# Attention weights turned by VectorE in 32x32 blocks after a pass through DRAM, in place of eight TensorE transposes per head

## The chip, the core and the metric

The kernel runs on one core of a Trainium2 chip. TensorE multiplies matrices (PE in the profile, with its weight loads as PEld), VectorE (DVE) and ScalarE (ACT) work on tiles in on-chip memory, GpSimd (POOL) does little here, and SyncE (SP) issues most DMAs. Engines work through their instructions in order and meet by semaphores. An instruction that waits therefore holds everything that stands behind it on its engine, DMAs that this engine issues included. TensorE writes to eight PSUM banks, each 128 partitions by 512 values.

The metric is the device time of one execution in microseconds (us); lower is better. Three runs of the kernel before took 1805.0, 1805.11 and 1809.3 us, so the median is 1805.11 us. The profiled execution is a fourth one.

## The reference

Two layers over 256 latent tokens (a grid of 4 rows by 64) and 256 context tokens, width 2048. The first layer projects the tokens by one large matrix into queries, keys, values, gates and the inputs of a state space model (SSD), lets 16 attention heads and the SSD work beside each other, and projects both results back. The second is a short gated convolution. The change lies in the attention of the first layer:

```python
s_lat = jnp.einsum('bqhd,bkhd->bhqk', qr, kb).astype(jnp.float32) * scale + bias.astype(jnp.float32)
s_lat = jnp.where(mask, s_lat, -jnp.inf)
s_ctx = jnp.einsum('bqhd,bkhd->bhqk', qr, k_ctx).astype(jnp.float32) * scale
pr = jax.nn.softmax(jnp.concatenate([s_lat, s_ctx], axis=-1), axis=-1).astype(v.dtype)
return (jnp.einsum('bhqk,bkhd->bqhd', pr[..., :kh * GRID_W], vb)
        + jnp.einsum('bhqk,bkhd->bqhd', pr[..., kh * GRID_W:], v_ctx))
```

With four grid rows every query sees all 256 latent keys (those out of its column window are masked) and the 256 context keys. So a head has a 256 x 512 matrix of weights. The attention output is then multiplied by a SiLU gate: `ya = ya * jax.nn.silu(...)`.

## The kernel before

**Precision.** A product of two float32 tiles is made of three TensorE matmuls: each operand is split into a rounded high part H (a cast, mostly on ScalarE) and a remainder L (a subtraction on VectorE), and H·H, L·H and H·L are summed in a bank. For the large weights this runs as a stream. SyncE loads 512 KB into one of five `raw` buffers, ScalarE casts it to `wH` (L409), VectorE subtracts to `wL` (L416), TensorE uses both. There are three pairs `wH`/`wL`, so a cast waits until TensorE is done with the chunk three back.

**Order.** The program is written out by a planner in the code: the class `Plan` keeps a clock for each engine, to which the method `cost` adds an estimate for each instruction. Generators (`head_gen`, `kq_gen`, `mix_gen` and others) yield conditions; `may` lets one go on when its inputs are ready by those clocks, when a bank is free (`nb=1`), and when the budget of ten `tmp` tiles of 128x512 and nine `half` tiles allows it (`grow` asks for tiles, `cap` gives the claim back). The planner fixes only the order in which each engine gets its instructions and which buffer they use; on the chip each starts when its real inputs are there. The conditions named "AQ" stand for DMAs that ScalarE issues (`DMA2`).

**The projections.** Columns of the input projection come in four groups `a`, each with K, Q, G (gate) and V of four heads, and between them the SSD groups with columns B, C, X and Z. The SSD columns go through `conv`: one activation from the bank (L1194), four multiply-adds on VectorE that read the same bank (L1200), a tanh (L1203) and a last multiply-add (L1207). `kq_gen` normalises K and Q into six `tmp` tiles and then turns each by four TensorE transposes into a bank (`turn`, L202); ScalarE copies the four turned K tiles to `KT` (L962), VectorE the two of Q to `QT` (L964). It does the turning for group `a` only when `attn[0] >= 8 * a`, that is, when all heads of the earlier groups are done, because there is one `KT` and one `QT`. V and G wait for the same in their banks.

**A head.** `head_gen(a, h)` splits K and Q, makes two score tiles (128 queries by 512 keys each), adds the bias and takes the row maximum (`top`), applies the exponential on ScalarE with the row sum, and scales by 0.5 over the sum on VectorE (`scale_`, L1028 and L1029). Then the weights are turned, since the next product sums over keys: `trans` makes four TensorE transposes per score tile into a bank, ScalarE casts the bank to half of `PH` (L1065), VectorE subtracts to half of `PL` (L1067). After the split of V (`vH`, and `vL` in L1076) twelve matmuls of 256 columns sum the head's output (the PV product below), VectorE multiplies by the gate (L1087), and `put_mix` writes the result to DRAM by a DMA that ScalarE issues (L921).

**The output projection.** `mix_gen` reads two heads back from DRAM (L1516), splits them (L1521, L1522), and the output projection uses them as `mix0` to `mix31` (16 attention heads, 16 halves of the SSD). Heads 12 to 15 are the last ones that it uses, `mix12` to `mix15`.

## Time and profile before

| Quantity | Value |
| --- | --- |
| Median of three runs | 1805.11 us |
| Profiled execution, its own time | 1800.62 us |
| Span of that profile | 1798.8 us |
| Granted TensorE clock, mean | 0.999 |
| TensorE matmuls on `tmp` tiles by L202 (transposes) | 324 |
| of these in the attention heads, 16 x 8 | 128 |
| ScalarE busy, share of the span | 44% |
| VectorE busy, share of the span | 72% |

The span goes from the first to the last instruction; the rest of the execution's time, 1.8 us, lies around it. A busy time is a sum of durations on the engine, with overlapping ones counted once. A matmul's duration runs from its start to its modelled end and overlaps the next one's, so the pace of TensorE is read from starts, not from means. "Idle before" is the time in which the engine had nothing to do ahead of a group, with what ended it.

The attention lies between about 200 and 1240 us of the span.

### The profile page before, as it was taken

What the parts mean: (1) busy time and instruction counts of PE and PEld (TensorE: products, weight loads), DVE (VectorE), ACT (ScalarE), POOL (GpSimd) and SP (SyncE); (2) the same over time, 40 slices, a digit from 0 to 9 for tenths busy, and PEclk for the clock granted to TensorE, in tenths of its full rate; (3) what the DMA queues carried; (4) which work ended last, traced back from release to release, by engine and by line L of the source; (5) the groups of instructions that cost most, each with busy time, mean ns of one, the idle gap of its engine ahead of it and who ended that gap; (6) DMA issues with size and microseconds to landing.
All of it is one profiled execution on the core that took longest, in us unless ns stands there. A gap on an engine that the chain in (4) does not pass through costs nothing.

```text
span 1798.8 us, 26647 instructions
## 1 busy us (share of the span) xinstructions
PE 1765.1 (98%) x10057; PEld 1493.6 (83%) x10057; DVE 1302.0 (72%) x2121; ACT 796.7 (44%) x1410; POOL 31.1 (2%) x28
## 2 busy tenths in 40 slices
PE   6999999999999999999999999999999999999998
PEld 4677888888888879888888898888878888888887
DVE  5566777878686877685875787787657777777665
ACT  5322544436252455242454343654445444444442
POOL 0000100001000000000001000000000000000000
PEclk9999999999999999999999999999999999999999
DMA  9987654566656556655574566878857777877564
GB/s 343 343 289 256 194 168 126 156 205 196 201 171 190 156 184 200 191 157 167 171 218 119 163 190 194 233 218 286 282 182 229 242 247 226 263 224 247 188 210 153
DMA packets 249217, 376.92 MB, mean 210 GB/s; under 512 B 32656, under 2 KB 104048, under 8 KB 249088
## 3 DMA queue, kind: packets, MB, share of 16 engines
q1 hardware_dynamic: 239792, 366.64, 65.5%
q10 hardware_dynamic: 9296, 8.57, 1.4%
q8 instruction: 79, 1.29, 0.3%
q14 instruction: 50, 0.41, 0.1%
HBM read 368.70 MB, written 7.77 MB: 209 GB/s over the span
## 4 chain that ended last, share of the span: by engine, by line
PE 91%; DMA 3%; DVE 3%; issue 1%; ACT 1%; SPq 0%; POOL 0%; POOLq 0%; DVEq 0%; ACTq 0%
PE bank L198 89%; PE bank L202 3%; DMA tmp<-dram_csr 2%; DVE wL L416 1%; DMA raw<-in_ada_w 0%; DMA tmp<-dram_mixd 0%; DVE acc L803 0%; DMA tmp<-in_x 0%; DVE hL L752 0%; SPq L566 0%; DVE tmp L1381 0%; DVE tmp L1200 0%; ACT wH L409 0%; DVE half L1396 0%; DVE tmp L748 0%
## 5 line engine op out<-in xcount | busy, mean ns | idle before, releaser
L409 ACT CAST wH<-raw 128x1024 fp32r<-128x1024 f32 (+1 forms) x440 | 459.1, 1044 | 684.7 <-PE bank L198 585.5
L416 DVE TENSOR_TENSOR wL<-raw,wH 128x1024 fp32r<-128x1024 f32 (+1 forms) x440 | 531.9, 1214 | 227.0 <-ACT wH L409 224.3
L198 PE MATMUL bank<-h,wH 128*128 128x512 f32 x1024 | 358.7, 395 | 2.7 <-ACT h L1664 1.5
L198 PE MATMUL bank<-hH,wH 128*128 128x256 f32 (+1 forms) x1040 | 343.2, 330 | 0.9 <-ACT wH L409 0.9
L198 PE MATMUL bank<-hL,wH 128*128 128x256 f32 (+1 forms) x1040 | 337.2, 324 | 0.0
L198 PE MATMUL bank<-hH,wL 128*128 128x256 f32 (+1 forms) x1024 | 331.7, 324 | 1.1 <-DVE wL L416 1.1
L198 PE MATMUL bank<-h,wL 128*128 128x256 f32 x1024 | 287.2, 280 | 0.1
L198 PE MATMUL bank<-wH,hH 128*128 128x512 f32 x640 | 257.4, 403 | 4.8 <-ACT hH L746 2.6
L198 PE MATMUL bank<-wL,hH 128*128 128x512 f32 x640 | 250.1, 391 | 0.3 <-DVE wL L416 0.3
L198 PE MATMUL bank<-wH,hL 128*128 128x512 f32 x640 | 249.8, 391 | 0.1
L803 DVE SCALAR_TENSOR_TENSOR acc<-raw,csil,acc 128x512 f32<-128x512 f32 x256 | 191.8, 749 | 59.8 <-DMA raw<-in_ada_w 45.4
L198 PEld LDWEIGHTS bank<-h,wH 128*128 128x128 f32 x1024 | 192.2, 188 | 48.4 <-issue 2.6
L198 PEld LDWEIGHTS bank<-hH,wH 128*128 128x128 f32 x1040 | 197.9, 190 | 18.7 <-issue 2.0
L198 PEld LDWEIGHTS bank<-hL,wH 128*128 128x128 f32 x1040 | 198.0, 190 | 15.4
L198 PEld LDWEIGHTS bank<-hH,wL 128*128 128x128 f32 x1024 | 194.8, 190 | 17.5 <-DVE wL L416 2.1
L198 PEld LDWEIGHTS bank<-h,wL 128*128 128x128 f32 x1024 | 193.6, 189 | 0.4 <-DVE wL L416 0.4
L198 PE MATMUL bank<-wH,mix 128*128 128x512 f32 x512 | 162.8, 393 | 0.0
L198 PEld LDWEIGHTS bank<-wH,hH 128*128 128x128 f32 x640 | 120.3, 188 | 35.3 <-issue 6.6
L198 PEld LDWEIGHTS bank<-wH,hL 128*128 128x128 f32 x640 | 120.2, 188 | 25.4 <-DVE hL L752 0.6
L198 PEld LDWEIGHTS bank<-wL,hH 128*128 128x128 f32 x640 | 120.3, 188 | 24.6 <-DVE wL L416 1.1
L198 PEld LDWEIGHTS bank<-wH,mix 128*128 128x128 f32 x512 | 96.2, 188 | 20.7 <-issue 0.9
L198 PE MATMUL bank<-wL,mix 128*128 128x512 f32 x256 | 99.9, 390 | 0.0
(259 smaller groups left out, 1790.1 us busy)
## 6 DMA issues: line engine op xcount, KB each, us to landing
raw<-in_w_in SPq DMA_DIRECT2D x209, 512.0 KB
raw<-in_ada_w SPq DMA_DIRECT2D x163, 512.0 KB
raw<-in_sc_in SPq DMA_DIRECT2D x128, 512.0 KB
raw<-in_w_out SPq DMA_DIRECT2D x64, 512.0 KB
raw<-in_sc_out SPq DMA_DIRECT2D x32, 512.0 KB
tmp<-dram_csr SPq DMA_DIRECT2D x32, 256.0 KB
PT<-in_ada_w SPq DMA_DIRECT2D x14, 512.0 KB
yi<-in_ada_w SPq DMA_DIRECT2D x8, 512.0 KB
```

The lines of the kernel that those rows point to most:

```text
L198: E(T.matmul(o, l, r, start=start, stop=stop, skip_group_check=True))
L202: E(T.transpose(o, i, ident if k == 128 else ident[:k, :k]))
L409: E(S.copy(H, v))
L416: E(V.tensor_tensor(out=Lo, in0=v, in1=H.bitcast(F32), op=ALU.subtract))
L803: E(V.scalar_tensor_tensor(out=acc, in0=v[:, j], scalar=csil[:, 2 * k + j:2 * k + j + 1], in1=acc, op0=ALU.mult, op1=ALU.add))
```

## The change

Per head, the eight transposes, the bank they took, two casts and two subtractions go. In their place:

- The exponential writes into a new `tmp` tile with its columns in another order (`mixed`): the columns of key block k, 32-wide piece b, move so that DRAM rows can be read in whole pieces of 128 values.
- The scaling goes from VectorE to ScalarE (`S.mul`), and its factor 0.5 goes into the gate multiplication, now a `scalar_tensor_tensor`.
- ScalarE's queue writes each scaled tile to DRAM (`ptd`, 256 KB, two per head). `fetch` reads them back with four DMAs, each to 32 partitions, eight pieces of 512 bytes for each partition: 4 x 32 x 8 = 1024 pieces per head.
- `blocks` turns the fetched tile by a VectorE transpose that works in 32x32 blocks, two instructions of 128x512 per head, into `Pf`.
- One cast of 128x1024 makes `PH`, one subtraction of 128x1024 makes `PL`.
- A head asks for three `tmp` tiles rather than two, and gives its claim back before the fetch rather than after the turning.
- The planner's cost list treats the new transpose like a reduction.

```diff
-            if op in ("Reciprocal", "TensorReduce"):
+            if op in ("Reciprocal", "TensorReduce", "StreamTranspose"):
...
+    mixed = lambda ap: ap.rearrange("p (b k i) -> p k b i", b=4, k=4)
+    plain = lambda ap: ap.rearrange("p (k b i) -> p k b i", b=4, k=4)
+
+    def fetch(dst, src):
+
+        n = src.shape[0] // 32
+        for b in range(4):
+            E(DMA2.dma_start(dst[32 * b:32 * b + 32].rearrange("p t (a x) -> p (t a) x", a=4),
+                             bass.AP(tensor=src.tensor, offset=src.offset + 128 * b, ap=[[512, 32], [32 * 512, n], [1, 128]])))
+
+    def blocks(o, i):
+
+        E(V.transpose(o.rearrange("p k (a j) -> p a k j", a=4), i.rearrange("p (a k j) -> p a k j", a=4, k=4)))
...
-    PH, PL = (st([128, 4, 256], f"PT{k}", F32R, name=f"P{'HL'[k]}") for k in range(2))
+    PH = st([128, 4, 256], "PH", F32R)
+    Pf = st([128, 4, 256], "PT1", name="Pf")
+    ptd = drt([16, 256, 512], "ptd")
...
-            E(S.activation(sp, sp, AF.Exp, bias=s4[:, 2 + qt:3 + qt], scale=1.0, accum_out=s4[:, 4 + qt:5 + qt]))
+            ex = sps[qt] = tmp()
+            E(S.activation(mixed(ex), plain(sp), AF.Exp, bias=s4[:, 2 + qt:3 + qt], scale=1.0, accum_out=s4[:, 4 + qt:5 + qt]))
+            give(free_t, sp)
 
         def scale_(qt):
-            sp = sps[qt]
+            yield W_("DVE", s4[:, 4 + qt:5 + qt])
             E(V.reciprocal(s4[:, 6 + qt:7 + qt], s4[:, 4 + qt:5 + qt]))
-            E(V.tensor_scalar(out=sp, in0=sp, scalar1=s4[:, 6 + qt:7 + qt], scalar2=0.5, op0=ALU.mult, op1=ALU.mult))
-
-        def trans(qt):
-            pt = bank()
-            for kt in range(4):
-                turn(pt[:, kt * 128:(kt + 1) * 128], sps[qt][:, kt * 128:(kt + 1) * 128])
+            yield W_("ACT", s4[:, 6 + qt:7 + qt])
+            E(S.mul(sps[qt], sps[qt], s4[:, 6 + qt:7 + qt]))
+            yield W_("AQ", sps[qt])
+            E(DMA2.dma_start(ptd[hd, qt * 128:(qt + 1) * 128], sps[qt]))
             give(free_t, sps[qt])
-            return pt
...
-        yield ("grow", 2, 0)
+        yield ("grow", 3, 0)
...
+        for qt in range(2):
+            yield from scale_(qt)
+        yield ("cap", 0, 0)
         yield when(lambda: hd == 0 or ("pv", hd - 1) in got)
+        yield W_("AQ", ptd[hd])
+        Dt = st([128, 2, 512], "PT0", name=f"D{hd}")
+        fetch(Dt, ptd[hd])
         for qt in range(2):
-            yield W_("PE", sps[qt], nb=1)
-            pt = trans(qt)
-            t = slice(qt * 128, (qt + 1) * 128)
-            yield W_("ACT", pt)
-            E(S.copy(PH[:, :, t], four(pt)))
-            yield W_("DVE", PH[:, :, t])
-            E(V.tensor_tensor(out=PL[:, :, t], in0=four(pt), in1=PH[:, :, t].bitcast(F32), op=ALU.subtract))
-            give(free_b, pt)
-        yield ("cap", 0, 0)
+            yield W_("DVE", Dt)
+            blocks(Pf[:, :, qt * 128:(qt + 1) * 128], Dt[:, qt])
+        yield W_("ACT", Pf)
+        E(S.copy(PH, Pf))
+        yield W_("DVE", PH)
+        PL = st([128, 4, 256], "PT0", F32R, name=f"PL{hd}")
+        E(V.tensor_tensor(out=PL, in0=Pf, in1=PH.bitcast(F32), op=ALU.subtract))
...
-            E(V.tensor_tensor(out=o, in0=po[:, :256], in1=gt[:, h, :], op=ALU.mult))
+            E(V.scalar_tensor_tensor(out=o, in0=po[:, :256], scalar=0.5, in1=gt[:, h, :], op0=ALU.mult, op1=ALU.mult))
```

The planner writes another order with these estimates. Three places show it. Line numbers after the change are 14 or 15 higher at these places (before L409, L416, L921, L962, L1194, L1516; after L423, L430, L935, L976, L1209, L1531).

**First place: the end of head 3 and the turning of K and Q for the second group.** TensorE, before: `tmp` tiles are turned in banks 4, 7 and 1, each its own, with matmuls of the projection between (`hH10`, `hL10` are the split activations, `wH2`, `wL2` the split weights).

```order
L202 MATMUL bank4_127<-const_153,tmp7_111 128x128 x4
L198 MATMUL bank6_129<-hH10_1128,wH2_138 128x256
L198 MATMUL bank6_129<-hL10_1133,wH2_138 128x256
L198 MATMUL bank6_129<-hH10_1128,wL2_141 128x256
L198 MATMUL bank6_129<-hH10_1128,wH2_138 128x256
L198 MATMUL bank6_129<-hL10_1133,wH2_138 128x256
L198 MATMUL bank6_129<-hH10_1128,wL2_141 128x256
L202 MATMUL bank7_130<-const_153,tmp8_112 128x128 x4
L202 MATMUL bank1_124<-const_153,tmp4_108 128x128 x4
L198 MATMUL bank0_123<-hH11_1135,wH2_138 128x256
```

TensorE, after: the last rows of head 3's PV product (`PH`, `PL3`, `vH`, `vL`), the six turnings, and the first rows of the next projection.

```order
L198 MATMUL bank3_126<-PH_1685,vH_1690 128x256
L198 MATMUL bank3_126<-PL3_4050,vH_1690 128x256
L198 MATMUL bank3_126<-PH_1685,vL_1691 128x256
L202 MATMUL bank3_126<-const_153,tmp1_105 128x128 x4
L202 MATMUL bank3_126<-const_153,tmp2_106 128x128 x4
L202 MATMUL bank3_126<-const_153,tmp8_112 128x128 x4
L202 MATMUL bank3_126<-const_153,tmp4_108 128x128 x4
L202 MATMUL bank3_126<-const_153,tmp0_104 128x128 x4
L202 MATMUL bank3_126<-const_153,tmp7_111 128x128 x4
L198 MATMUL bank3_126<-hH0_360,wH2_138 128x256
```

The turnings now stand in one row with nothing between, all six in bank 3, directly behind head 3's PV product, which is in bank 3 too; the matmuls that stood between them come earlier.

VectorE, after, around the same place: the multiply-adds of `conv` read banks 3 and 7 (L1215), `half2` is head 3's gate multiplication (L1102), `QT` the copies of turned Q.

```order
L1215 SCALAR_TENSOR_TENSOR tmp5_109<-bank3_126,cwh_1672,tmp5_109 128x2x254
L430 TENSOR_TENSOR wL1_140<-raw0_131,wH1_137 128x1024
L1215 SCALAR_TENSOR_TENSOR tmp5_109<-bank3_126,cwh_1672,tmp5_109 128x2x255 x2
L1215 SCALAR_TENSOR_TENSOR tmp5_109<-bank3_126,cwh_1672,tmp5_109 128x2x254
L1222 SCALAR_TENSOR_TENSOR tmp5_109<-tmp6_110,tmp5_109 128x512
L1215 SCALAR_TENSOR_TENSOR tmp3_107<-bank7_130,cwh_1672,tmp3_107 128x2x254
L1215 SCALAR_TENSOR_TENSOR tmp3_107<-bank7_130,cwh_1672,tmp3_107 128x2x255 x2
L1215 SCALAR_TENSOR_TENSOR tmp3_107<-bank7_130,cwh_1672,tmp3_107 128x2x254
L1102 SCALAR_TENSOR_TENSOR half2_116<-bank3_126,gt_145 128x256
L978 TENSOR_SCALAR QT_143<-bank3_126,gqk_1678 128x4x128 x2
```

Head 3's product, the gate and the turnings follow a `conv` whose input lies in the same bank 3; ScalarE has ahead of that `conv` a cast to `wH1`, and behind it the tanh, the activation from bank 7 and the four copies to `KT`, in this order:

```order
L423 CAST wH1_137<-raw0_131 128x1024
L1209 ACTIVATE tmp5_109<-bank3_126,cbh_1674,cwh_1672 128x512
L1218 ACTIVATE tmp6_110<-tmp5_109 128x512
L1209 ACTIVATE tmp3_107<-bank7_130,cbh_1674,cwh_1672 128x512
L976 COPY KT_142<-bank3_126 128x4x128 x4
```

Before, casts of weights stood between those copies, which came from banks 1, 4, 7 and 1.

**Second place: the turning for the third group.** TensorE, after: head 7's PV product ends in bank 3, the two tiles of Q are turned in banks 5 and 3, and an SSD product uses bank 5 next.

```order
L198 MATMUL bank3_126<-PL7_5645,vH_1690 128x256
L198 MATMUL bank3_126<-PH_1685,vL_1691 128x256
L202 MATMUL bank5_128<-const_153,tmp1_105 128x128 x4
L202 MATMUL bank3_126<-const_153,tmp3_107 128x128 x4
L198 MATMUL bank5_128<-tmp8_112,xtm_147 64x128
```

The four tiles of K follow a little later, in banks 2 and 7 by turns.

```order
L198 MATMUL bank0_123<-wH1_137,hL0_364 128x512
L202 MATMUL bank2_125<-const_153,tmp7_111 128x128 x4
L202 MATMUL bank7_130<-const_153,tmp2_106 128x128 x4
L202 MATMUL bank2_125<-const_153,tmp1_105 128x128 x4
L202 MATMUL bank7_130<-const_153,tmp0_104 128x128 x4
L198 MATMUL bank4_127<-wH1_137,hH0_360 128x512
```

Before, the four tiles of K of this group were turned in banks 3, 4, 7 and 3, with matmuls of the projection between the first three.

**Third place: head 15 and the end of the output projection.** TensorE, before: the last rows of head 15's product stand ahead of `mix18`.

```order
L198 MATMUL bank5_128<-PH_1685,vH_1689 128x256
L198 MATMUL bank5_128<-PL_1686,vH_1689 128x256
L198 MATMUL bank5_128<-PH_1685,vL_1690 128x256
L198 MATMUL bank2_125<-wH1_137,mix18_9245 128x512
L198 MATMUL bank2_125<-wL1_140,mix18_9245 128x512
```

TensorE, after: the last rows of the same product, whose twelve rows follow directly on the last matmul on `mix13`, and the first rows on `mix14`, which is head 14 and, like `mix15`, comes back by the read that also waits for head 15.

```order
L198 MATMUL bank0_123<-PH_1685,vH_1690 128x256
L198 MATMUL bank0_123<-PL15_10046,vH_1690 128x256
L198 MATMUL bank0_123<-PH_1685,vL_1691 128x256
L198 MATMUL bank4_127<-wH2_138,mix14_10067 128x512
L198 MATMUL bank4_127<-wL2_141,mix14_10067 128x512
```

ScalarE, after: the fetch of head 15 (`D15` from `ptd`), four casts of weights, the split of the turned weights and of V, the write of head 15's result and the read of both heads.

```order
L212 DMA D15_9972<-dram_ptd_1687 32x8x128 x4
L423 CAST wH1_137<-raw4_135 128x1024
L423 CAST wH2_138<-raw1_132 128x1024
L423 CAST wH0_136<-raw3_134 128x1024
L423 CAST wH1_137<-raw2_133 128x1024
L1081 CAST PH_1685<-Pf_1686 128x1024
L1089 CAST vH_1690<-Vt_144 128x512
L935 DMA dram_mixd_1684<-half5_119 128x256
L1531 DMA tmp5_109<-dram_mixd_1684 128x2x256
L1536 CAST mix14_10067<-tmp5_109 128x256
```

Head 15 has moved from well ahead in the output projection to the place right in front of its first use; between its product and that use nothing is left on TensorE.

More of the change, by code (lines that the diff above doesn't have):

```diff
@@ L1054, in head_gen @@
         yield from top(1, p1)
-        yield W_("DVE", sps[0])
-        scale_(0)
-        yield W_("DVE", sps[1])
-        scale_(1)
+        for qt in range(2):
+            yield from scale_(qt)
+        yield ("cap", 0, 0)
         yield when(lambda: hd == 0 or ("pv", hd - 1) in got)
+        yield W_("AQ", ptd[hd])
+        Dt = st([128, 2, 512], "PT0", name=f"D{hd}")
+        fetch(Dt, ptd[hd])
         for qt in range(2):
-            yield W_("PE", sps[qt], nb=1)
-            pt = trans(qt)
-            t = slice(qt * 128, (qt + 1) * 128)
-            yield W_("ACT", pt)
-            E(S.copy(PH[:, :, t], four(pt)))
-            yield W_("DVE", PH[:, :, t])
-            E(V.tensor_tensor(out=PL[:, :, t], in0=four(pt), in1=PH[:, :, t].bitcast(F32), op=ALU.subtract))
-            give(free_b, pt)
-        yield ("cap", 0, 0)
+            yield W_("DVE", Dt)
[5 more added lines that the diff above has]
+        E(V.tensor_tensor(out=PL, in0=Pf, in1=PH.bitcast(F32), op=ALU.subtract))
         yield when(lambda: ("V", a) in got and ("G", a) in got)
```

## The prediction

> **What bounds the kernel now.** The busy times come first, at the head of the page; of a row, the busy us, the share of the span and the instructions:

> ```profile
> PE 1765.1 (98%) x10057; PEld 1493.6 (83%) x10057; DVE 1302.0 (72%) x2121; ACT 796.7 (44%) x1410; POOL 31.1 (2%) x28
> ```

> TensorE is busy for 98%. Next, the view by windows, for the stretch in which the attention lies; after the length come busy us of PE, PEld, DVE, ACT and POOL, the granted clock, the DMA share and GB/s.

> ```profile
> 200.00:1240.00 1040.00, 1036.40 (x5938) 892.42 (x5937) 784.28 (x1344) 468.63 (x929) 27.04 (x16) 1.00 0.62 186
> ```

> Here TensorE lacks 3.6 us of 1040. So in this stretch every us of TensorE work that goes is a us won, as long as nothing makes TensorE wait, and every wait of TensorE is lost in full: there is no slack to take it back. ScalarE (469 us busy) and VectorE (784 us) have room on average. Whether TensorE waits is decided by the order in single places.

> **What the change removes.** The chain of waits in order of time (start, us, what) shows what a transpose costs; below it the group of all transposes of `tmp` tiles (busy us, mean ns of one, then idle before).

> ```profile
> 15.82 4.57 PE bank L202 x32
> ...
> 276.26 0.87 PE bank L202 x8
> ...
> L202 PE MATMUL bank<-const,tmp 128*128 128x128 f32 x324 | 45.9, 273 | 0.2 <-ACT KT L962 0.2
> ```

> The mean of 273 ns is a duration up to a modelled end and overlaps its neighbours; a row of eight takes 0.87 us, 109 ns each. For 16 heads with 8 transposes each that is 128 x 109 ns = **14.0 us** less. [...]

> **What it adds beside TensorE.** The groups by form, with mean ns of one behind the busy us:

> ```profile
> L416 DVE TENSOR_TENSOR wL<-raw,wH 128x1024 fp32r<-128x1024 f32 x433 | 527.0, 1222 | 226.3 <-ACT wH L409 223.6
> L409 ACT CAST wH<-raw 128x1024 fp32r<-128x1024 f32 x433 | 454.8, 1051 | 666.9 <-PE bank L198 573.8 <-issue 58.2 <-DMA bias<-dram_rpbs 5.7
> L1067 DVE TENSOR_TENSOR PL<-bank,PH 128x512 fp32r<-128x512 f32 x32 | 21.9, 686 | 6.1 <-ACT PH L1065 5.7
> L1065 ACT CAST PH<-bank 128x512 fp32r<-128x512 f32 x32 | 18.2, 586 | 30.5 <-PE bank L202 29.0 <-DVE half L1087 1.5
> L1029 DVE TENSOR_SCALAR tmp<-tmp,s 128x512 f32<-128x512 f32 x32 | 15.6, 487 | 1.1
> L596 ACT ACTIVATE xs<-xs,rx 128x512 f32<-128x512 f32 x8 | 5.4, 716 | 5.8 <-POOL rx L555 5.8
> L793 DVE MEMSET acc<- 128x512 f32 x16 | 7.8, 485 | 0.9
> L964 DVE TENSOR_SCALAR QT<-bank,gqk 128x512 f32<-128x512 f32 x8 | 5.8, 747 | 2.2 <-PE bank L202 2.2
> ```

> The issue rows of ScalarE's writes and SyncE's small-piece reads give min, median and max ns of issuing:

> ```profile
> L921 ACTq DMA_DIRECT2D dram_mixd<-half x32: 321/328/623, 285.9 to 1217.5; - x32
> ...
> L1001 SPq DMA_DIRECT2D bias<-dram_rpbs x64: 573/614/1828, 229.1 to 1166.3; - x64
> ```

> The block transpose of 128x512 is in no row. The cheapest and the dearest VectorE pass of that size shown here take 0.485 (a fill) and 0.747 us (from a bank); I take 0.6, between them, as it reads on-chip memory. VectorE per head: minus 2 x 0.487 (scaling) and 2 x 0.686 (`PL` halves), plus 1.222 (`PL` whole) and 2 x 0.6, so +0.1 us. ScalarE per head: plus 2 x 0.716 (scaling), 1.051 (cast), 2 x 0.328 (writes), 4 x 0.614 (fetch), minus 2 x 0.586, so +4.4 us, 71 us in all, on an engine with 571 us free in the stretch. Both I cost at nothing: casts of weights mostly wait for TensorE (574 of 667 idle us in L409's row), so this work fits into waits. If that cover were gone for a head, up to 4.4 us would show there. The trip through DRAM lies between scores and product, where TensorE has tens of us of projection for most heads.

> **First stop: head 3's product and the turning for the second group.** The order puts the product, then all six turnings in bank 3, with nothing between; the bank's earlier user is a `conv`. More groups, then TensorE's timeline at head 15's product, and the gate on VectorE behind it:

> ```profile
> L1194 ACT ACTIVATE tmp<-bank,cbh,cwh 128x512 f32<-128x512 f32 x24 | 18.0, 767 | 0.0
> L1200 DVE SCALAR_TENSOR_TENSOR tmp<-bank,cwh,tmp 128x510 f32<-128x510 f32 x48 | 35.9, 747 | 1.3
> L1200 DVE SCALAR_TENSOR_TENSOR tmp<-bank,cwh,tmp 128x508 f32<-128x508 f32 x48 | 35.4, 744 | 3.6 <-ACT tmp L1194 3.1
> L1203 ACT ACTIVATE tmp<-tmp 128x512 f32<-128x512 f32 x24 | 15.1, 629 | 7.0 <-DVE tmp L1200 7.0
> L1207 DVE SCALAR_TENSOR_TENSOR tmp<-tmp,tmp 128x512 f32<-128x512 f32 x24 | 16.4, 684 | 0.0
> L1087 DVE TENSOR_TENSOR half<-bank,gt 128x256 f32<-128x256 f32 x16 | 6.7, 422 | 9.7 <-PE bank L198 9.7
> L962 ACT COPY KT<-bank 128x512 f32<-128x512 f32 x16 | 8.9, 589 | 8.7 <-PE bank L202 8.7
> ```

> ```profile
> 1195.65 0.28 PE L198 MATMUL bank<-PH,vH 128*128 128x256 f32 x1
> ...
> 1196.94 0.28 PE L198 MATMUL bank<-PH,vL 128*128 128x256 f32 x1
> 1197.05 0.40 PE L198 MATMUL bank<-wH,mix 128*128 128x512 f32 x1
> ```

> ```profile
> 1197.43 0.42 DVE L1087 TENSOR_TENSOR half<-bank,gt 128x256 f32<-128x256 f32 x1
> ```

> The twelve rows of a product take 1197.05 - 1195.65 = 1.40 us. Let TensorE reach head 3's product at 0, when it has just freed `wH1`. ScalarE's queue then has the cast (to 1.05) and the activation of `conv` (to 1.82); VectorE does one multiply-add (to 2.56), `wL1` (to 3.78) and three more (2 x 0.747 + 0.744, to 6.02). With 0.2 for handovers bank 3 is free at 6.2. Then the tanh (0.63), the last multiply-add of `conv` (0.68) and, beside it, the activation from bank 7 (0.77), four multiply-adds (2.98) and the gate (0.42) follow, for the gate stands behind them on VectorE: 11.2. The product itself lies beside these. The six turnings are one chain, since each needs the bank back: 6 x 0.44 on TensorE, 2 x 0.747 and 4 x 0.589 for the copies, together 6.5, and handovers of 0.27 each, taken between nothing and the 0.49 us from the product's last start (1196.94) to the gate's (1197.43): 8.1, end at 19.3. TensorE works for 1.40 + 2.62 of it, so it stands for **15.3 us** (bounds 13.5 to 16.7 by the handovers). Before, the turnings used several banks and had projection between them, so all this was hidden. What is queued behind: the casts for the next weights, which TensorE needs only after the stop.

> **Third group.** Head 7's product is followed by Q's turnings in banks 5 and 3 and an SSD product in bank 5. Bank 3 waits for the gate (0.49 - 0.12 + 0.42 behind the product, less the 0.44 of the other turning: 0.4), bank 5 for gate and copy on VectorE: 1.0 more. K's tiles alternate between two banks and lose about 0.4 twice. Together **2.2 us**, between 0 and 4.4.

> **Second stop: head 15 ahead of `mix14`.** The rows of ScalarE's timeline give the latency of a read-back, from issue to the first cast, at three places, and the write of head 15:

> ```profile
> 1103.67 0.37 ACTq L1516 DMA_DIRECT2D tmp<-dram_mixd  x1
> ...
> 1106.33 0.71 ACT L1521 CAST mix<-tmp 128x256 fp32r<-128x256 f32 x2 [0.55 <-DMA tmp<-dram_mixd]
> ...
> 1142.89 0.41 ACTq L1516 DMA_DIRECT2D tmp<-dram_mixd  x1
> ...
> 1147.14 0.71 ACT L1521 CAST mix<-tmp 128x256 fp32r<-128x256 f32 x2 [0.31 <-DMA tmp<-dram_mixd]
> ...
> 1199.33 0.34 ACTq L921 DMA_DIRECT2D dram_mixd<-half  x1
> ...
> 1209.22 0.38 ACTq L1516 DMA_DIRECT2D tmp<-dram_mixd  x1
> ...
> 1216.98 0.41 ACT L1521 CAST mix<-tmp 128x256 fp32r<-128x256 f32 x1 [4.37 <-DMA tmp<-dram_mixd]
> ```

> ```profile
> L1076 DVE TENSOR_TENSOR vL<-Vt,vH 128x512 fp32r<-128x512 f32 x16 | 10.9, 684 | 0.1
> L1521 ACT CAST mix<-tmp 128x256 fp32r<-128x256 f32 x32 | 11.1, 402 | 10.5 <-DMA tmp<-dram_mixd 10.5
> ```

> The latencies are 2.7, 4.3 and 7.8 us. Before, head 15's write stood 10 us ahead of the read, and TensorE had other halves to work on. After, TensorE reaches head 15's product at 0 having just freed `wH1`: cast (to 1.05), `wL1` (to 2.27) with `PH`'s cast beside it, `PL` (to 3.49), `vL` (to 4.17), with handovers 4.5. Product 1.40 (to 5.9), handover and gate 0.8 (6.7), issue of the write 0.33, its landing, the read, the cast 0.40. A write's landing is in no row; I take the shortest read, 2.7, between nothing and 4.3. With a read of 4.3 the first matmul on `mix14` starts at 14.3, and TensorE stands for 14.3 - 1.4 = **12.9 us** (8.7 with no landing and a read of 2.7; 18.0 with 4.3 and 7.8).

> **Work behind a stop.** The chain's first row above has 32 transposes in 4.57 us, right after TensorE's wait at the start; at 109 ns they would take 3.49. So a long wait costs 1.1 us afterwards; for two stops **2.2 us**, between 0 and the rival below.

> **Sum.** -14.0 + 15.3 + 2.2 + 12.9 + 2.2 = +18.6 us on the profiled execution's own 1800.62, so 1819.2. The median of the runs lies 4.5 above that execution; against the median the forecast is **1823.7 us**. Its own bounds (each term's, most of them at once being unlikely) give 1816 to 1830.

> **Rivals.**

> - *TensorE works slowly through the stops.* Products and turnings inside them are 1.40 + 2.62 + 1.40 = 5.4 us of work; at half pace they add 5.4: 1829.1. For it: the slow start-up row. Against it: the granted clock is 1.00 in the window, though its idle time, 3.6 us in all, hardly tries it. [...]
> - *The fetched pieces come late.* 1024 pieces per head, on queues busy with weights; with 7.8 instead of 4.3 us VectorE waits at the block transposes, `wL` is queued behind them and TensorE waits for it. At two heads with little room (15, whose product has 8 to 10 us of TensorE work behind its fetch, and one more) that is 2 x 3.5: 1830.7. For it: the 7.8 us read. Against it: most heads have over 12 us there (both counted in the new order at this profile's pace of TensorE).
> - *One stop only.* If ScalarE and VectorE are so far ahead that the second stop is hidden, 12.9 + 1.1 fall away: 1809.7. Within 0.3% of the median (5.4 us, about what a measurement of this kernel can tell from no change) is where all stops together cost 8.6 to 19.4 us.
> - *Faster.* The planner's rows only set an order. If `conv` and the gate are done when TensorE arrives, because TensorE is later there than the planner thinks, the stops vanish: 1805.1 - 14.0 = 1791.1. It decides below 8.6 us of stops. For it: L1087's gate waits for TensorE in most of its idle time. Against it: the cast to `wH1` can't start before TensorE frees that buffer, so the chain of the first stop can't run ahead.
> - *The removal pays nothing*, as the transposes filled gaps anyway: 1837.7. Against it: 3.6 us idle in 1040.

> **Chances.** Forecast 0.48, slow work 0.17, late pieces 0.13, one stop 0.12, faster 0.07, no pay 0.03. Faster by over 0.3%: 0.07; within: 0.12; slower: 0.81. The range 1810 to 1837 takes in the first three cases with their bounds and leaves out the most of the others.

> **What would show it.** Transposes of `tmp` tiles: 196 rather than 324. At the first stop an idle time of about 6 us before the product and gaps of near 1 us between six turnings. Idle time of about 8 us before the first `mix14`, with a read-back ahead of it. A block transpose near 0.6 us, hardly any wait for `ptd` on VectorE. A clock below 1.00 behind the stops would speak for slow work. Wrong is the prediction if the turnings run without gaps, or if TensorE's idle time is spread over many heads.

## The result, and the profile after

The changed kernel took 1835.72 us (median of four runs, 1834.53 to 1839.31); the kernel before, run beside it, 1807.2 us. The ratio is 1.016 with a 95% interval of 1.014 to 1.0179: 28.5 us slower. The forecast was +18.6 us, 1823.7. The profiled executions lie a little further apart: 1835.04 and 1800.62 us, with spans of 1833.2 and 1798.8.

The head of the page after:

```profile
span 1833.2 us, 26538 instructions
...
PE 1766.5 (96%) x9929; PEld 1486.6 (81%) x9929; DVE 1301.6 (71%) x2105; ACT 814.1 (44%) x1426; POOL 36.5 (2%) x28
```

TensorE has 128 matmuls fewer (9929 for 10057) and yet 1.4 us more busy time, and its idle time went from 1798.8 - 1765.1 = 33.7 to 1833.2 - 1766.5 = 66.7 us. So two things are to be found: where 33.0 us of new idle time lie, and why its work takes longer in busy time by some 15 us than the removed transposes allow. (A busy time counts each matmul to its modelled end, so some of the latter are ends that overlap nothing now.)

The windows view answers the first. Of the kernel before, three stretches (length, then busy us of PE, PEld, DVE, ACT, POOL, granted clock, DMA share, GB/s):

```profile
450.00:550.00 100.00, 100.00 (x533) 85.03 (x532) 76.14 (x123) 38.70 (x62) 0.00 (x0) 1.00 0.60 183
700.00:750.00 50.00, 50.00 (x278) 42.96 (x277) 34.37 (x59) 19.40 (x30) 0.00 (x0) 1.00 0.56 172
1150.00:1300.00 150.00, 150.00 (x719) 124.18 (x718) 115.58 (x176) 76.38 (x118) 1.43 (x2) 1.00 0.79 256
```

The same stretches of the changed kernel:

```profile
450.00:550.00 100.00, 87.58 (x433) 72.65 (x432) 57.58 (x97) 36.99 (x59) 1.61 (x1) 0.88 0.49 147
700.00:750.00 50.00, 44.52 (x304) 38.25 (x304) 45.06 (x91) 31.82 (x90) 4.75 (x3) 1.00 0.65 187
1150.00:1300.00 150.00, 135.36 (x620) 109.94 (x619) 104.13 (x171) 72.73 (x121) 2.26 (x2) 0.95 0.75 237
```

12.4, 5.5 and 14.6 us of idle time, 32.5 of the 33.0, lie in three stretches: the three places of the order that the prediction named. In two of them the granted clock is down as well (0.88 and 0.95).

**The first stop**, TensorE's timeline (start, us, what; in brackets the idle time before and what ended it):

```profile
502.01 0.39 PE L198 MATMUL bank<-hH,wL 128*128 128x512 f32 x1
508.22 0.55 PE L198 MATMUL bank<-PH,vH 128*128 128x256 f32 x1 [5.82 <-DVE tmp L1215]
508.57 0.41 PE L198 MATMUL bank<-PL,vH 128*128 128x256 f32 x1
508.78 0.41 PE L198 MATMUL bank<-PH,vL 128*128 128x256 f32 x1
...
512.98 1.11 PE L202 MATMUL bank<-const,tmp 128*128 128x128 f32 x4 [1.86 <-DVE half L1102]
514.94 1.12 PE L202 MATMUL bank<-const,tmp 128*128 128x128 f32 x4 [0.84 <-DVE QT L978]
...
518.69 1.12 PE L202 MATMUL bank<-const,tmp 128*128 128x128 f32 x4 [0.68 <-ACT KT L976]
...
524.07 0.58 PE L198 MATMUL bank<-hH,wH 128*128 128x256 f32 x1 [0.68 <-ACT KT L976]
```

And the granted clock in it, from the windows view:

```profile
508.30:513.00 4.70, 2.83 (x13) 2.54 (x13) 3.99 (x6) 1.16 (x2) 0.00 (x0) 0.50 0.42 114
...
524.00:528.00 4.00, 3.93 (x18) 3.93 (x19) 1.68 (x3) 4.00 (x10) 0.00 (x0) 0.50 0.09 33
528.00:532.00 4.00, 4.00 (x37) 3.63 (x35) 1.24 (x3) 2.73 (x6) 0.00 (x0) 0.87 0.00 0
```

This is the predicted chain: the product waits 5.8 us for the last multiply-add of `conv` in its bank, the first turning for the gate, each next one for the copy out of the same bank. What the forecast had too small is the pace. A product's matmuls start 0.21 us apart instead of 0.12, four transposes, 0.44 us by their pace before, take 1.11 up to their modelled end, and the clock stays at 0.50 until about 5 us after work has become continuous again at 524.07 (0.87 as the mean of 528 to 532 us puts its return at 529).

**The last stop**, pieces of the chain of waits in order of time:

```profile
1244.89 5.28 DMA dram_mixd<-half
...
1250.19 0.31 ACTq L212
...
1250.54 8.84 DMA D<-dram_ptd
...
1264.37 2.51 PE bank L198 x10
...
1267.36 1.69 DMA dram_mixd<-half
...
1269.07 3.44 DMA tmp<-dram_mixd
```

The pieces of the last of head 15's four fetch DMAs land 8.84 us after that DMA was issued. TensorE is done with `mix13` at 1258.43 and waits for them and for the block transposes, the cast and the subtraction behind them; then the product, the gate, the write and the read of the result follow one by one. The first two lines say that the third DMA of that fetch went out only when the write of an earlier result had landed.

One wait was in no term of the sum. These are SyncE's and ScalarE's timelines around the fetch of head 14 (what is issued on their queues is marked SPq and ACTq), and the row of all issues of the fetch (min, median and max ns):

```profile
1218.78 0.37 SPq L393 DMA_DIRECT2D raw<-in_w_out  x1
...
1219.72 1.64 ACTq L212 DMA_DIRECT2D D<-dram_ptd  x3
...
1227.42 0.31 ACTq L212 DMA_DIRECT2D D<-dram_ptd  x1
1227.83 1.04 ACT L423 CAST wH<-raw 128x1024 fp32r<-128x1024 f32 x1 [7.12 <-PE bank L198]
...
L212 ACTq DMA_DIRECT2D D<-dram_ptd x64: 309/462/1648, 280.2 to 1250.5; - x64
```

Three of the four DMAs go out in 1.64 us. The fourth starts 6.06 us later, and the cast to `wH` stands behind it on ScalarE. It isn't the issuing that takes long: no issue of the fetch takes more than 1.65 us. By the semaphore events in the trace, the fourth DMA waits for the very semaphore that will tell of its own landing, and that one was still counting the weights that SyncE had asked for at 1218.78. They had landed at 1227.40, 22 ns before the fourth DMA started. (The view puts the cast's wait down to TensorE, but the next cast follows without a wait, so buffers were free.) TensorE then stood for 1.14 and 0.76 us. In three more places, not counting this one, the waits view puts casts down to the fetch directly (us in total, times, longest):

```profile
ACT wH L423 <- DMA D<-dram_ptd: 18.0, 3, 7.9
```

### The profile page after: what moved, and what is told of

Read it like the earlier page. It is cut to its first block, busy times and chain, and to the rows that moved or that the text cites. A ratio compares the mean times of both kernels' runs of the same rounds, so it can differ in the third digit from the quotient of the medians.

```text
span 1833.2 us, 26538 instructions
## 1 busy us (share of the span) xinstructions
PE 1766.5 (96%) x9929; PEld 1486.6 (81%) x9929; DVE 1301.6 (71%) x2105; ACT 814.1 (44%) x1426; POOL 36.5 (2%) x28
## 4 chain that ended last, share of the span: by engine, by line
PE 89%; DMA 4%; DVE 4%; ACT 1%; issue 1%; POOL 0%; ACTq 0%; SPq 0%; DVEq 0%; POOLq 0%
PE bank L198 87%; PE bank L202 2%; DVE wL L430 1%; DMA D<-dram_ptd 1%; DMA raw<-in_ada_w 1%; DMA dram_mixd<-half 0%; ACT wH L423 0%; DMA tmp<-dram_csr 0%; DVE acc L817 0%; DMA raw<-in_w_in 0%; POOL statk L569 0%; DMA raw<-in_w_out 0%; DVE tmp L1215 0%; DMA xs<-in_x 0%; DVE hL L766 0%
## 5 line engine op out<-in xcount | busy, mean ns | idle before, releaser
L423 ACT CAST wH<-raw 128x1024 fp32r<-128x1024 f32 (+1 forms) x440 | 458.6, 1044 | 689.0 <-PE bank L198 540.9
L430 DVE TENSOR_TENSOR wL<-raw,wH 128x1024 fp32r<-128x1024 f32 (+1 forms) x440 | 530.4, 1212 | 223.4 <-ACT wH L423 214.2
L198 PE MATMUL bank<-h,wH 128*128 128x512 f32 x1024 | 360.4, 397 | 2.6 <-ACT h L1679 1.5
L198 PE MATMUL bank<-hH,wH 128*128 128x256 f32 (+1 forms) x1040 | 341.9, 329 | 1.6 <-ACT wH L423 0.9
L198 PE MATMUL bank<-hL,wH 128*128 128x256 f32 (+1 forms) x1040 | 337.8, 325 | 0.0
L198 PE MATMUL bank<-hH,wL 128*128 128x256 f32 (+1 forms) x1024 | 332.2, 324 | 3.9 <-DVE wL L430 3.9
L198 PE MATMUL bank<-h,wL 128*128 128x256 f32 x1024 | 286.3, 280 | 0.4 <-DVE wL L430 0.4
L198 PE MATMUL bank<-wH,hH 128*128 128x512 f32 x640 | 257.1, 402 | 6.7 <-ACT hH L760 2.6
L198 PE MATMUL bank<-wL,hH 128*128 128x512 f32 x640 | 249.9, 391 | 1.0 <-DVE wL L430 1.0
L198 PE MATMUL bank<-wH,hL 128*128 128x512 f32 x640 | 249.7, 391 | 0.1
L198 PEld LDWEIGHTS bank<-h,wH 128*128 128x128 f32 x1024 | 192.2, 188 | 50.8 <-issue 2.6
L198 PEld LDWEIGHTS bank<-hH,wH 128*128 128x128 f32 x1040 | 198.8, 191 | 20.0 <-issue 2.3
L198 PEld LDWEIGHTS bank<-hH,wL 128*128 128x128 f32 x1024 | 195.6, 191 | 20.5 <-DVE wL L430 5.3
L198 PEld LDWEIGHTS bank<-hL,wH 128*128 128x128 f32 x1040 | 198.9, 191 | 15.5
L198 PEld LDWEIGHTS bank<-h,wL 128*128 128x128 f32 x1024 | 193.0, 188 | 0.7 <-DVE wL L430 0.7
L198 PE MATMUL bank<-wH,mix 128*128 128x512 f32 x512 | 162.9, 394 | 8.7 <-ACT mix L1536 7.6
L198 PEld LDWEIGHTS bank<-wH,hH 128*128 128x128 f32 x640 | 120.2, 188 | 37.6 <-issue 6.1
L198 PEld LDWEIGHTS bank<-wL,hH 128*128 128x128 f32 x640 | 120.2, 188 | 26.2 <-DVE wL L430 2.5
L198 PEld LDWEIGHTS bank<-wH,hL 128*128 128x128 f32 x640 | 120.1, 188 | 25.6 <-DVE hL L766 0.6
L198 PEld LDWEIGHTS bank<-wH,mix 128*128 128x128 f32 x512 | 96.9, 189 | 30.6 <-ACT mix L1536 8.3
L198 PE MATMUL bank<-wL,mix 128*128 128x512 f32 x256 | 100.6, 393 | 1.1 <-DVE wL L430 1.1
```

The source lines that it names most:

```text
L198: E(T.matmul(o, l, r, start=start, stop=stop, skip_group_check=True))
L423: E(S.copy(H, v))
L430: E(V.tensor_tensor(out=Lo, in0=v, in1=H.bitcast(F32), op=ALU.subtract))
```

## The experiments

The theory: the order that the planner wrote makes TensorE stop in those three places, and these stops, with the slow clock in and behind them, are the loss. The main rival: the transfers themselves (their pieces, their landing, their issue on ScalarE) cost the time wherever they stand. All ratios below are to the kernel before, which ran beside each group (medians 1805 to 1807).

| Run | Median us | Ratio (95%) |
| --- | --- | --- |
| changed kernel | 1835.72 | 1.016 (1.014 to 1.0179) |
| landing estimate altered | 1831.0 | 1.0125 (1.0101 to 1.0148) |
| and earlier start of scores | 1820.15 | 1.007 (1.0047 to 1.0092) |
| before, transposes doubled | 1813.45 | 1.0038 (1.0026 to 1.0051) |
| changed, useless matmuls in the last stop | 1834.04 | 1.0152 (1.013 to 1.0173) |
| changed, without the trip | 1810.55 | 1.0026 (1.0012 to 1.0039) |
| fetch issued by GpSimd | 1867.85 | 1.0348 (1.0312 to 1.0383) |
| before, heads planned late | 1856.88 | 1.0271 (1.0237 to 1.0304) |
| changed, late results not through DRAM | 1820.97 | 1.0071 (1.0049 to 1.0093) |
| three edits together | 1813.98 | 1.0035 (1.0021 to 1.0049) |
| before, late results not through DRAM | 1805.85 | 0.9993 (0.998 to 1.0007) |
| changed, late results direct, heads first | 1808.83 | 1.0018 (0.9999 to 1.0038) |
| late results direct, landing estimate altered | 1829.6 | 1.0125 (1.0109 to 1.0141) |

**The last stop.** The edit, in the method that writes a head's or an SSD half's result:

```diff
     def put_mix(i, o):
+        if free_rows[0] > i % 16:
+            yield W_("ACT", o)
+            split_mix(i, o)
+            give(free_h, o)
+            written.add(i)
+            return
         yield W_("AQ", o)
```

`split_mix` makes the cast and the subtraction of `mix_gen`, now from the half tile on chip. On the changed kernel:

> The changed kernel, with one edit at its end: results that are ready once the activations' rows are free (heads 12 to 15 and late SSD halves) are split straight from their half tile into the mix tile, without the write to DRAM and the read back. In the changed kernel's chain that pair of DMAs takes 1.69 + 3.44 us between head 15's gate and the split, and the earlier pair held ScalarE too. Theory (the last stop's greater part is this read-back directly ahead of its use): the idle time ahead of mix14 falls from 6.4 us to about 1.5, its slow clock behind goes: 6 to 10 us less, 1826 to 1830. Rival (TensorE is held there by the weights, not by the read-back): within 3 us of 1835.7.

The same edit on the kernel before, as a control:

> The kernel before with the same edit at its end alone (no read-back for late results). It has no stop there, so the theory expects no change: 1803 to 1809. If it becomes faster by more than 5 us, the edit helps by itself and is no measure of the last stop.

14.75 us went, half again the most that was expected, and the control did not move. The stretch that had 14.6 us of idle time has 4.8, with the clock at 1.00:

```profile
1150.00:1300.00 150.00, 145.22 (x681) 119.22 (x681) 112.12 (x178) 79.68 (x127) 1.83 (x2) 1.00 0.79 250
```

So the way of late results through DRAM is the greater part of the last stop, the slow clock included. That is more than the read-back alone: the write that held head 15's fetch went too, and with it TensorE's wait ahead of that head's product. The two parts aren't told apart.

**The first and the middle stop.** One more edit on that kernel:

```diff
         if s:
+            if s < 3:
+                force(lambda: attn[0] >= 8 * s)
             psB = banks(2)
             proj(256, 512, psB, 1)
```

> The kernel of the run without the read-back of late results, with one more edit: before the projection of the SSD columns B of groups 1 and 2 takes its two banks, what is left of the heads of the group ahead is written out. Head 3's product then stands at 430 us of TensorE work instead of 451, ahead of that projection and of its conv, and the six turnings of K and Q alternate between banks 7 and 3. Theory (the first stop is the conv in the same bank and the one bank for six turnings): of 19.5 us lost between 500 and 550 us some 2 to 5 remain, of 7.6 between 700 and 750 some 2: 1821.0 - 20 = about 1801 us (1796 to 1808), at or below the kernel before. Rival (head 3's data are not there earlier, so TensorE waits for the fetch at the new place instead): 1815 to 1825.

12.1 us went. The median, 1808.83, is just above the theory's range, and can't be told from the kernel before. The same two stretches:

```profile
450.00:550.00 100.00, 94.81 (x489) 78.72 (x489) 69.18 (x114) 41.75 (x65) 1.61 (x1) 0.97 0.63 188
700.00:750.00 50.00, 50.00 (x295) 43.11 (x294) 34.55 (x72) 25.22 (x44) 1.43 (x2) 1.00 0.70 221
```

The idle time fell from 12.4 to 5.2 and from 5.5 to nothing. What remains at the first place is of another kind, in the chain of waits at 480 us: head 3's block transposes stand on VectorE behind multiply-adds of the second layer's vector work, which wait for their weights (6.28 and 4.46 us in that chain), and the product waits for them. So TensorE does wait for head 3's data at the new place, as the rival said, though not for the fetch.

With the first two edits of the planner alone, the other way to move the heads, the outcome was worse than the theory said. In the planner's clock, the landing of a DMA that ScalarE issues no longer stands behind SyncE's weight loads:

```diff
-                done = free = max(self.dma, s + 1000) + n / self.RATE + 1500
+                done = free = s + 1000 + n / self.RATE + 1500
```

> The changed kernel with one line of the planner's clock altered: the landing of a DMA that ScalarE issues no longer stands behind the weight loads in SyncE's queue. Work and data are the same, only the order differs: head 3's product stands 83 us of TensorE work earlier (369 instead of 451 us), and the turnings of K and Q for groups 1 and 2 use three or four banks with projection between. Theory (the order makes the stops): the first stop (about 22 us lost at 502 to 528 us of the changed kernel's profile) and the third group's (about 6 us) go, the one at head 15 stays: 1835.7 - 22 - 6 = about 1808 us (1803 to 1814). Rival (the transfers themselves, their 1024 pieces per head and their issue on ScalarE, cost the time): within 5 us of 1835.7.

And with a head's scores allowed to start earlier:

```diff
-        yield when(lambda: hd < 2 or ("pv", hd - 2) in got)
+        yield when(lambda: hd < 2 or ("sm", hd - 2) in got)
```

(`"sm"` is set when both tiles of the softmax are written.)

> As the run with the altered landing estimate, and a head may start its scores when the softmax of the head two before is written, not only when that head's product is. Head 15's product then stands at 1121 us of TensorE work instead of 1143, and the first matmul on mix14 some 20 us behind it. Theory: the last stop goes too (about 19 us in the changed kernel's profile), and the 14.0 us of the removed transposes show: 1807 - 14 = 1793 us (1789 to 1799), faster than before. Rival (transfers cost the time): above 1815. Rival (transposes were hidden, their removal pays nothing): 1807.

Both fell short of the theory's figure, by 23 and 27 us, and both times lie where the main rival put them. The stops of groups 1 and 2 went as expected, but others came. In the second run, two places from the chain of waits:

```profile
516.31 5.65 DMA raw<-in_ada_w
...
1142.92 9.55 DMA tmp<-dram_mixd
```

The first is VectorE waiting for weights of its own vector work, with `wL` queued behind it; the other is a read-back of results. The three edits together:

> Altered landing estimate, earlier start of scores, and no read-back for late results, together. Theory (what is lost beside the stops in the run with the first two is mostly the read-back of results, 21 us of ScalarE waiting for it): 1805 to 1813, about the kernel before. If the removed transposes show in full: 1795. Rival (losses move on to the next narrow place): 1815 to 1822, as without it.

That was 1813.98, 0.35% above before and between the two ranges. And the altered estimate with the late results direct:

> The run with the altered landing estimate alone, without the read-back of late results. Theory (that run lost its gain at the end, where 14.5 and 8.6 us went from 1200 to 1300 us, at read-backs): 1831.0 - 20 = about 1811 (1803 to 1816). Rival (its other losses, 9.0 us between 850 and 900 and 8.1 between 1150 and 1200, are of another kind and stay, and more come): 1817 to 1828.

It took 1829.6 us, 1.6 above the rival's range. In this order head 15's fetch stood so close ahead of its product that VectorE waited for it, and TensorE with it (14.4 us ahead of the product):

```profile
DVE Pf L217 <- DMA D<-dram_ptd: 12.3, 1, 12.3
```

Against the main rival as it was put, that the transfers cost the time wherever they stand, is the 1808.83 us of the run with late results direct and heads first: it makes every transfer of the trip, and ScalarE issues them. But it also has the 128 transposes less, so what the trip still costs there is about what they are worth.

**Order alone.** In the kernel before, only the planner's clock for the weights was set back:

```diff
     attn = [0]
+    LATE = 30000.0
...
         yield when(lambda: hd == 0 or ("pv", hd - 1) in got)
+        for k in plan.keys(sps[0]) + plan.keys(sps[1]):
+            plan.w[k] = max(plan.w[k], plan.t["ACT"] + LATE)
```

> The kernel before with its own work, only the planner is told that a head's weights are ready for turning 30 us later than it thinks. Instructions and data are the same, the order is not: head 15's product stands directly ahead of mix14, and the turnings of group 1 stand in a row in two banks. Theory (order alone makes the stops): about 13 us at mix14 with the slow clock behind it, and 2 to 5 us at the turnings: 1815 to 1828. Rival (it needs the trip through DRAM): within 5 us of 1807.

It lost 51.6 us, with the same instructions and no trip for the weights. The size was missed, the direction not: beside the read-back ahead of `mix14` there was a wait of the product for `PL`, which stood on VectorE behind multiply-adds that waited for their weights four times (3.6 to 5.9 us), of which the last in the chain:

```profile
1269.45 3.60 DMA raw<-in_ada_w
...
1274.69 1.21 DVE PL L1070 x2
```

**The trip.** Without it (the edit takes out the writes and `fetch`, gives the tiles to `blocks` where they are, and keeps a claim of two `tmp` tiles until then):

> The changed kernel without the trip: neither the writes to ptd nor the fetch; VectorE turns the scaled tiles where they are, in 32x32 blocks, so the weights are not fully turned and the output is not the reference's. All other work of the change stays: scaling on ScalarE, block transposes, wide cast and subtraction, three tmp tiles. The order comes out near that of the kernel before (head 15's product at 1111 us of TensorE work, head 3's at 340). Theory (what costs is that the trip makes heads late in the order): no stops, and the removed transposes show by what the run with doubled transposes gave, 6.7 (to 14.0) us: 1793 to 1801. Rival (the new work on ScalarE and VectorE costs too): 1807 or above.

1810.55, above the theory's range and inside the rival's. A new stop of the known kind holds the largest part: TensorE stands for 9.35 us between 1200 and 1250 us, where results go through DRAM (first the window, then the chain of waits):

```profile
1200.00:1250.00 50.00, 40.65 (x181) 32.96 (x180) 30.97 (x49) 19.52 (x30) 0.69 (x1) 0.90 0.78 263
...
1225.56 6.22 DMA dram_mixd<-half
...
1231.89 5.32 DMA tmp<-dram_mixd
```

So 25 us of the changed kernel's loss go with the trip, and even without it a new order took away much of what the transposes gave. That the work on ScalarE and VectorE has a small part in the rest isn't excluded.

**Who issues.** `DMA2` became GpSimd's queue for the writes and the fetch:

> The kernel of the run with the earlier start of a head's scores, with the writes to ptd and the fetch issued by GpSimd, which is idle 98% of the span, instead of ScalarE. In that run ScalarE's casts to wH waited 20.5 us in five places for the fetch's DMAs to be issued. The order also moves head 15's product forward to 1097 us of TensorE work. Theory (the rest of the loss is ScalarE held at the issue of the fetch, with casts queued behind, and heads that are late for it): 1795 to 1805, at or below the kernel before. Rival (landing of the pieces, or contention of their descriptors with weight loads, whoever issues them): 1815 to 1825 as with ScalarE. Rival (GpSimd's issue takes long): slower, with the block transposes waiting for the fetch.

Much slower, the outcome that the last rival named, though a single issue isn't long. The block transposes wait for the fetch, and within head 13's fetch GpSimd stands for 3.83 us ahead of the fourth DMA:

```profile
DVE Pf L217 <- DMA D<-dram_ptd: 69.7, 11, 9.4
...
1213.19 0.58 POOL L212 DMA_DIRECT2D D<-dram_ptd  x1 [3.83 <-issue]
```

An issue takes GpSimd 0.59 us by the median, and in all 16 heads the fourth DMA starts 0.3 us after the first has landed, 1.1 to 4.8 us behind the third. Besides, the fetch of a head can start only after the product of the head ahead, as its buffer is that head's `PL`, and within the later groups the products of neighbouring heads start only 10.4 to 18.5 us apart. Each link (issue, landing, two block transposes, cast, subtraction) then shows in full: behind the fourth issue at 792.50 us the last four took 4.79, 1.32, 1.05 and 1.24 us. How much of the loss each of the two makes isn't told apart.

**The price of a transpose.**

```diff
-            for kt in range(4):
+            for kt in (0, 1, 2, 3, 0, 1, 2, 3):
                 turn(pt[:, kt * 128:(kt + 1) * 128], sps[qt][:, kt * 128:(kt + 1) * 128])
```

> The kernel before, with every transpose of attention weights done twice into the same place, so 128 more transposes and nothing else. Price of 109 ns each (the pace in the chain of waits): 14.0 us more than before, 1821 us. Price of 273 ns each (the mean in the group's row): 35 us more, 1842. Transposes hidden in gaps: no change, 1807.

The median rose by 6.7 us (4.7 to 9.2 by the interval), less than 14.0; but TensorE's busy time shows about the forecast's figure:

```profile
span 1811.0 us, 26906 instructions
...
PE 1778.4 (98%) x10185; PEld 1505.6 (83%) x10185; DVE 1298.5 (72%) x2121; ACT 797.7 (44%) x1410; POOL 32.2 (2%) x28
```

Busy time rose by 13.3 us. From the first start of each row of `tmp` transposes to the next start behind it, all rows together take 31.0 us before and 45.0 us here, 14.0 more. The price of 273 ns each is excluded. The span rose by 12.2, but that is no second proof: the profiled execution of the kernel before is 6.1 us below the median of its runs here, and the one with doubled transposes 0.7 below. Less 5.4 for that, it is 6.8, about what the medians show. Why half of the added work is not in the time stays open; part of the transposes may fill waits that this one execution of the kernel before did not have.

**The clock.** Useless matmuls (20 ahead of head 15's product, 30 behind it) in the changed kernel:

> The changed kernel with 20 useless matmuls of 512 columns on TensorE ahead of head 15's product and 30 between it and the first matmul on mix14, where TensorE otherwise stands. Theory (the clock falls because TensorE stands, and costs about 2 us behind the stop and 1.4 in the product): the product runs at about 117 ns per matmul instead of 213 and the matmuls on mix14 at 227 instead of 427, with the granted clock at 1.00 there; the end comes about 2 to 3.5 us earlier, less what the useless matmuls run over (20 x 0.227 = 4.5 and 30 x 0.227 = 6.8 us, in stops of 4.0 and 6.4): 1832 to 1837 us. Rival (the slow pace comes from the operands just written or the transfers, not from standing): paces of 213 and 427 ns stay.

TensorE's timeline there:

```profile
1267.17 0.27 PE L198 MATMUL bank<-PH,vH 128*128 128x256 f32 x1
1267.28 0.28 PE L198 MATMUL bank<-PL,vH 128*128 128x256 f32 x1
...
1267.87 6.98 PE L198 MATMUL bank<-kH 128*128 128x512 f32 x30
1274.68 0.39 PE L198 MATMUL bank<-wH,mix 128*128 128x512 f32 x1
1274.91 0.39 PE L198 MATMUL bank<-wL,mix 128*128 128x512 f32 x1
```

The product's matmuls start 0.11 to 0.12 us apart, the ones on `mix14` 0.23. In the changed kernel, same place:

```profile
1272.99 0.80 PE L198 MATMUL bank<-wH,mix 128*128 128x512 f32 x1 [6.12 <-ACT mix L1536]
1273.59 0.63 PE L198 MATMUL bank<-wL,mix 128*128 128x512 f32 x1
1274.01 1.05 PE L198 MATMUL bank<-wH,mix 128*128 128x512 f32 x2
```

There they are 0.42 to 0.43 us apart until 1276.56, for 3.6 us. The cast of `mix14` starts 0.46 us ahead of its first use in the changed kernel and 1.01 us ahead here, so the operands are about as new in both, and the slow pace comes from standing (6.12 us ahead of `mix14` there). The time, 1834.04, can't be told from that of the changed kernel.

## Why the prediction was right, point by point

**The places** were right: three stops, in the places of the order that were named, hold 32.5 of 33.0 us of new idle time, and two edits aimed at them gave back 14.75 and 12.1 of the 28.5 us. The figure was 9.9 us low: 1835.72 lies above the sum's own bounds (1816 to 1830), and within the stated range only because that one had been drawn wide enough for two rivals.

**Transposes, -14.0 us.** In TensorE's own time confirmed (14.0 us more from start to start, 13.3 busy, where they were doubled). In the median doubling cost 6.7, so the gain that was set against the stops may have been too large by half. The rival by which the removal pays nothing gave 1837.7, of all the nearest to the result; 4.7 to 9.2 us for the doubling speak against it in that form.

**Added work at nothing.** The block transpose took 0.688 us (0.6 was taken, within its bounds), ScalarE's scaling 0.720 (0.716). Hidden, as forecast, except around the fetch: an issue was taken at 0.614 us and took 0.462 by the median, but in head 14 the fourth DMA was held for 6.06 us, with a cast behind it. The rival of late pieces saw a wait on VectorE; here it came on ScalarE, and in another order on VectorE.

**First stop, 15.3 + 1.1 us.** TensorE finishes the projection at 502.24 (last start plus 0.23) and goes on at 524.07. Less 4.02 of work (1.40 and 2.62), that is 17.8 us, and about 2.3 more follow at half pace: 20.1. The chain ahead of the turnings took 10.7 us (11.2 forecast). The mis-sized term is the six turnings, 11.1 instead of 8.1 us, as the clock had fallen during the wait ahead (to 0.50 from 506 us on).

**Third group, 2.2 us** became 5.5, above its own bound of 4.4. In the chain of waits a cast on ScalarE stood behind a read of the SSD's, and the normalisation of K on VectorE behind `wL`, neither of them in the sum:

```profile
704.83 6.91 DMA tmp<-dram_csr
...
725.99 2.39 DVE tmp L959 x4
```

**Second stop, 12.9 + 1.1 us.** From 1258.43 to 1272.99, less 1.40 of work, is 13.2 us, and the eight slow matmuls behind it took 3.6 us instead of 1.8: 15.0. The size held (the recorded parts of 14.3 add up to 14.4), the parts differed: the wait ahead of the product was the fetch and not the chain from the cast to `wH`, and write and read took 1.69 and 3.44 us where 2.7 and 4.3 were taken.

**Slow work in the stops** was a rival at 0.17, and came true. It was priced at 1829.1, with half pace as an assumption that no row of the prediction shows; the trace after has a clock of 0.50. It also has 3.6 us of slow matmuls behind the last stop and about 5 behind the first. At the first stop TensorE's work ended at 502.24 us, and the granted clock was 1.00 until 504, 0.78 as the mean of 504 to 506 and 0.50 from there. How long a wait it takes isn't shown by the runs. With late results direct, the kernel before went to half pace behind a wait of 1.83 us (TensorE's timeline, then the window with the clock, 0.57 as its mean):

```profile
673.77 0.65 PE L198 MATMUL bank<-tmp,xtm 128*64 128x128 f32 x6 [1.83 <-DVE tmp L1397]
...
674.00:678.00 4.00, 4.00 (x15) 3.13 (x12) 3.97 (x10) 2.56 (x8) 0.00 (x0) 0.57 0.49 131
```

The profile of the kernel before could not show the price, since its longest wait after the start-up is 1.49 us.

So the mechanism was right and the sum too small by about 10 us: half pace inside the stops, a larger middle stop, and 3.4 us between 1200 and 1250 us, most of it (1.9) behind the held fetch of head 14. The parts found, 20.1 + 5.5 + 15.0 + 3.4 less 14.0, make 30.0 us, against 28.5 by the medians and 34.4 between the two profiled executions; 4.4 us of the latter are not located.

Still open is what would have to be done for the transposes' gain to show. The best version that keeps the change, 1808.83, equals the kernel before; in it casts stood longer behind the fetch than in the changed kernel:

```profile
ACT wH L423 <- DMA D<-dram_ptd: 43.0, 7, 9.7
```

These too are holds and not issues: up to 4.3 us ahead of a fetch's first DMA, for the product of the head ahead that still uses the buffer, and up to 4.6 us ahead of its fourth, for an earlier transfer's landing. A buffer of its own for the fetch was not tried, nor a way to keep its DMAs from waiting for transfers of the other queue while ScalarE issues them.

## What to carry to other kernels

Where one engine is busy 98% of the time and the others meet it in a fixed order, a change that adds latency to a side chain is priced in that order: look for the places where the late chain lands directly ahead of its use, or where several steps end up in one buffer, and add up those waits; work removed from the busy engine, here 14.0 us, is small beside two of them, here 20.1 and 15.0. A stop on TensorE can cost more than its length: here the work in it, and 3.6 to 5 us of work behind it, ran at half pace. And an edit that moves one stop away is only won if the new order is looked through again: most of the reordered versions here lost elsewhere a good part of what they gave back.
